# A decoder trunk on one core: TensorE's order in the first attention, and bias vectors made on 128 partitions

## The chip, the cores and the metric

The kernel runs on one core of a Trainium2 chip. The metric is device time in microseconds (us) of the whole program, from one launch; the median of three runs is given. TensorE does the matrix products (PE in the rows; PEld are its weight loads), VectorE (DVE), ScalarE (ACT) and GpSimd (POOL) work on rows of data, SyncE (SP) issues most transfers, and ScalarE's queue issues some. [...]

## The reference

Two layers on 512 rows of 1024 numbers, in float32. The first layer's mixer is an NSA (sparse attention with three branches: compressed, selected and window) beside a DSA (an index that picks the top 256 keys, then latent attention). The second is a differential attention. After each comes an MLP with a squared ReLU. A table of 32 distances x 16 heads is added to every softmax logit.

```python
h = modulate(x, sh1, sc1)                     # sh, sc, g from c @ ada_w + ada_b
...
nsa_q, kvc, kvs, kvw, gate, dsa_q, dsa_kv, idx_q, idx_k, idx_w = _split(h @ w_in, EVEN_SIZES)
o_a = nsa_attention(nsa_q, kvc, kvs, kvw, gate, ..., rel_bias[:, :NSA_HEADS])
o_b = dsa_attention(dsa_q, dsa_kv, idx_q, idx_k, idx_w, kv_norm, w_uk, w_uv, rel_bias[:, NSA_HEADS:])
y = jnp.concatenate([o_a, o_b], axis=-1) @ w_out
x = layer_norm(ALPHA * x + (1.0 + g1[:, None, :]) * y, ln_g[l, 0], ln_b[l, 0])
h = modulate(x, sh2, sc2)
y = jnp.square(jax.nn.relu(h @ w1)) @ w2
```

## The kernel before

Every float32 product with a weight is made as three matmuls of rounded numbers (`mm3`, L348 to L352): a value is kept as a high part (a cast, on ScalarE, L265) and a low part (value minus high part, on VectorE, L266), and high x high, high x low and low x high are added up in a PSUM bank.

`even` (L1030) is the first attention. It runs in these stages:

- **First projection** (L1045 to L1062): eight steps k. Step k loads a slice of ada_w and of ev_b1, makes `mod`, the high part of `hT` on ScalarE (L1051) and the low part on VectorE, and issues 24 matmuls of 512 columns and the like, into eight banks. The bias vectors are made in the meantime (`bias_vectors`, L587): `go` multiplies the table with a matrix of ones and zeros in five matmuls (L603), on 16 and 8 rows of output, and copies them to SBUF; `write` sends them to DRAM on ScalarE's queue, as `bvec` (16 heads, each repeated 23 times, 640 numbers) and `bdec` (8 heads, 8 times). It is called at k == 7, after the `hT` of that step. The repeats give every partition its own shifted copy when SyncE reads `g` from `bvec` (L537) and `ot` from `bdec` (L1214): those are the tables that are added to the scores.
- **Evacuation**: the key of the index and three of its four pairs of queries (`ik`, `iq`) are split into high and low parts (L372, L373, L472, L473), the values and the latent rows are copied (L529, L531, L1088), and `latent` (L1092 to L1100) normalizes the latent rows on VectorE; `latent_t` transposes them on TensorE (L1106).
- **A loop of 51 slots** (L1315). In each slot stand, in this order of the program: in the first 24, one unit of index scores (`idx`, scores at L504 and L505, VectorE's weighting at L1152 to L1157); then, from slot 15 on, NSA's units. Unit n has scores in slot n (`s0`: L504, L505, then the biased maximum on VectorE, L514), the division on GpSimd or VectorE one slot later (`s1`, L1277), the transposes two slots later (`s2`, L1479) and the products with the values four slots later (`pv`, L1297, L1305). Between these `fill.run` issues pieces of a queue, the **fill**: the remaining projections in the order iq, ks, kw, n0 to n3, kc, vc, the compression, and the DSA queries dq; `fill.share` says how much of it a slot gets. `topk` (L1183, L1184) adds rounds of VectorE's search for the largest index scores.
- **DSA** (L1375 to L1462): what is left of the fill, the products of the latent rows (`kproj`, Vd), and 16 units of the same kind, with the output projection of NSA's heads (eight pieces of 24 matmuls) as their fill.

The order of the instructions on each engine isn't that of the program. A scheduler walks the program and gives each engine the earliest instruction that is ready by its own model; so a matmul of the fill that stands later in the program is drawn ahead of scores that wait. Each engine's finished list is then fixed, and the chip runs it in that order.

SyncE loads weights 512 KB at a time into four buffers (`early_89`, `early_90`, `raw0_75`, `raw1_76`, L134). A buffer is free when the cast and the subtraction that read it are done, and SyncE's queue holds the loads in a fixed order, among them the loads of `g`.

Of the kernel before, what the change touches and what calls it, by code (L numbers as in the profile page):

```python
# [79 lines left out]
NREP = 23  # L80
# [207 lines left out]

class Fill:
# [37 lines left out]
class Trunk:  # L327
    def __init__(self, tc, a, out):
        self.tc, self.nc, self.a, self.out = tc, tc.nc, a, out
        self.lo_engine = "vector"  # L330
# [85 lines left out]
    def ada_pair(self, l, m, r0, r1):  # L416

        nc, mm = self.nc, self.nc.tensor.matmul
# [11 lines left out]
    def row(self, col, pool, tag, bufs=1):  # L430
# [3 lines left out]
        for h in range(2):  # L434
            ps = self.bank(self.row_tag)
            for k in range(4):
                c = 4 * h + k
                nc.tensor.matmul(ps[:, 128 * k:128 * k + 128], lhsT=col[:, c:c + 1].to_broadcast([128, 128]), rhs=self.ident,
                                 start=True, stop=True)
# [62 lines left out]
    def scores(self, ps, q, k, qs, ks, start=True):  # L502
        mm = self.nc.tensor.matmul
# [83 lines left out]
    def bias_vectors(self):  # L587
# [112 lines left out]
    def ln_b_(self, t, h, rows):  # L700

        nc, (_, cols) = self.nc, rows
        for kk in range(2):
            p = self.bank("t", (128, 4, 128))
            for k in range(4):
                nc.tensor.transpose(p[:, k, :], h[kk][:, 128 * k:128 * k + 128], self.ident)
# [323 lines left out]
    def even(self):  # L1030
# [14 lines left out]
        for k in range(8):  # L1045
# [14 lines left out]
            if k == 7:  # L1060
# [41 lines left out]
        def latent_t():  # L1102
            pt = self.bank("t")
            for t in range(4):
                ts = slice(128 * t, 128 * t + 128)
                nc.tensor.transpose(pt[:, ts], kv[:, ts], self.ident)  # L1106
# [112 lines left out]
        def cmp_a(k, i):  # L1219
# [6 lines left out]
            for s in range(4):  # L1226
                for o in range(0, 128, m):
                    nc.tensor.matmul(ps[o:o + m, 32 * s:32 * s + 32], lhsT=f32(nq[4 * k + s])[:, 128 * i + o:128 * i + o + m],
# [21 lines left out]
        def cmp_c(k, i, cb):  # L1250
            pt = self.bank("t")
            nc.tensor.transpose(pt[:, :128], cb, self.ident)
# [34 lines left out]
        def pv(n):  # L1287
# [6 lines left out]
            for br in range(2):  # L1294
                for j in range(i + 1):
                    for ab in range(2):
                        nc.tensor.matmul(o[ab], lhsT=V[:, br, j, 64 * ab:64 * ab + 64], rhs=pts[ab][br][:, 128 * j:128 * j + 128],  # L1297
# [16 lines left out]
        self.phase = "n"  # L1314
        for slot in range(end):  # L1315
# [74 lines left out]
        def s0(n):  # L1390
# [6 lines left out]
            for ab in range(2):  # L1397
                ps = self.bank("s")
                if i:
                    nc.tensor.matmul(ps[:, :w], lhsT=self.negr, rhs=drop[i][:, :w], start=True, stop=False)  # L1400
# [18 lines left out]
        def pv(n):  # L1419
# [3 lines left out]
            if p == 3:  # L1423
                po = self.bank("o")[:, :128]
                for j in range(i + 1):
                    c = (0, 128, 0, 384)[i] + 128 * j
                    for ab in range(2):
                        nc.tensor.matmul(po[64 * ab:64 * ab + 64], lhsT=Vd[:, j, p, 64 * ab:64 * ab + 64], rhs=PT[p][ab][:, c:c + 128],
# [16 lines left out]
        for n in range(N + e3):  # L1445
# [16 lines left out]
            st.pump(6)  # L1462
        self.phase = None
# [6 lines left out]
    def to_pt(self, i, zs, pts, c=None):  # L1470
# [5 lines left out]
        for z in zs:  # L1476
            t = self.bank("t")
            for j in range(i + 1):
                self.nc.tensor.transpose(t[:, 128 * j:128 * j + 128], z[:, 128 * j:128 * j + 128], self.ident)  # L1479
# [4 lines left out]
    def pv(self, po, pts, vs, half):  # L1484

        n = 4 if half else 2
        for j in range(n):
            both = j < n - 1
            for ab, (pt, v) in enumerate(zip(pts, vs)):
# [4 lines left out]
                self.nc.tensor.matmul(o if both else o[:, 128:], lhsT=v[j], rhs=y, start=j == 0, stop=j == n - 1)  # L1494
# [16 lines left out]
    def compress(self, kc, vc):  # L1511
# [4 lines left out]
        for kv in range(2):  # L1516
# [3 lines left out]
            for c in range(4):  # L1520
                w = st.get(I["cw1", kv, c])
                for li in range(4):
                    for k in range(2):
                        cs = 256 * li + 128 * k
                        for o in (0, 64) if 1 else (0,):
                            m = 64 if 1 else 128
                            nc.tensor.matmul(pss[k][o:o + m], lhsT=w[:, cs + o:cs + o + m], rhs=xl[:, :, 4 * c + li],
# [23 lines left out]
            for k in range(2):  # L1551
                if kv == 0:
                    nc.tensor.matmul(ps[:, :64], lhsT=w2[:, 128 * k:128 * k + 128],
# [369 lines left out]
```

## Time and profile before

| | |
|---|---|
| median of 3 runs | 1448.98 us (1446.71 to 1451.75) |
| the profiled execution | 1449.99 us; span of its instructions 1448.2 us |
| granted clock of TensorE, mean | 0.966 |
| VectorE busy | 1143.5 us (79%) |
| ScalarE busy | 658.8 us (45%) |
| GpSimd busy | 581.0 us (40%) |
| transfers | 189.47 MB, 131 GB/s on average |
| chain that ended last | TensorE 67%, VectorE 19%, DMA 4%, issue 4%, ScalarE 3%, GpSimd 2% |

A row of a timeline gives the start in us, how long the instruction or the group took, the engine and line, and in brackets how long the engine had been idle before and what ended that ("<-DVE q L373": it waited for VectorE's instruction of that line). [...] The profiled execution lies 1.0 us above the median.

### The profile page before, as it was taken

The page shows a single profiled execution, that of the slowest core. Times are in us where ns is not written, and L with a number is a line of the kernel's source. Part 1 is how long each engine was busy: PE and PEld are TensorE (multiplying, and loading weights), DVE is VectorE, ACT ScalarE, POOL GpSimd, SP SyncE. Part 2 cuts the span into 40 slices and gives each one's busy share as a digit, 9 for nine tenths or more (in the row PEclk, how much of TensorE's full clock was granted, in tenths as well). Part 3 has the DMA queues.
Part 4 walks back from the last instruction along what each step waited for, and adds up shares of the span by engine and source line. Part 5 has one row for each costly group of instructions (what it writes and reads, how often), then busy time and mean ns, then how long its engine had stood idle before and what let it go on. Part 6 is the DMA issues. An engine that isn't in the chain of part 4 may idle for free.

```text
span 1448.2 us, 22535 instructions
## 1 busy us (share of the span) xinstructions
PE 1342.0 (93%) x8286; PEld 1124.3 (78%) x8286; DVE 1143.5 (79%) x2185; ACT 658.8 (45%) x1412; POOL 581.0 (40%) x432
## 2 busy tenths in 40 slices
PE   6979998899899999999999799999979899999985
PEld 4758666676589888888887687887769789999974
DVE  6678979767578778878789825888975997898898
ACT  2455565746355333333332536776565443333321
POOL 2242677716432444444453622124164523122234
PEclk9989999999999999999999899999989999999997
DMA  9852432423731554444542442332350233323311
GB/s 333 247 165 94 152 104 90 131 72 106 258 132 37 183 178 172 175 175 161 189 163 91 149 153 92 102 103 78 137 166 14 90 100 117 110 70 113 116 59 58
DMA packets 58625, 189.47 MB, mean 131 GB/s; under 512 B 7778, under 2 KB 8482, under 8 KB 58516
## 3 DMA queue, kind: packets, MB, share of 16 engines
q1 hardware_dynamic: 55840, 184.67, 37.5%
q10 hardware_dynamic: 2676, 3.38, 1.1%
q8 instruction: 65, 1.06, 0.3%
q14 instruction: 44, 0.36, 0.1%
HBM read 178.42 MB, written 9.60 MB: 130 GB/s over the span
## 4 chain that ended last, share of the span: by engine, by line
PE 67%; DVE 19%; DMA 4%; issue 4%; ACT 3%; POOL 2%; SPq 0%; DVEq 0%; ACTq 0%; POOLq 0%
PE ps_mm L350 9%; PE ps_mm L351 9%; PE ps_mm L352 9%; PE ps_o L350 4%; PE ps_o L351 4%; PE ps_o L352 4%; PE ps_s L350 3%; PE ps_s L351 3%; PE ps_s L352 3%; PE ps_t L352 2%; PE ps_t L350 2%; PE ps_t L351 2%; DVE b L266 2%; PE ps_s L504 2%; PE ps_o L1297 2%
## 5 line engine op out<-in xcount | busy, mean ns | idle before, releaser
L350 PE MATMUL ps_mm<-hT,b 128*128 128x256 f32 (+1 forms) x560 | 190.9, 343 | 19.2 <-ACT b L265 13.1
L351 PE MATMUL ps_mm<-hT,b 128*128 128x256 f32 (+1 forms) x560 | 189.5, 339 | 5.4 <-DVE hT L717 5.1
L352 PE MATMUL ps_mm<-hT,b 128*128 128x256 f32 (+1 forms) x560 | 188.7, 338 | 1.8 <-DVE b L220 1.8
L350 PEld LDWEIGHTS ps_mm<-hT,b 128*128 128x128 f32 x560 | 108.5, 194 | 35.3 <-ACT b L265 13.1
L351 PEld LDWEIGHTS ps_mm<-hT,b 128*128 128x128 f32 x560 | 108.7, 194 | 18.1 <-DVE hT L717 5.6
L220 POOL TENSOR_TENSOR b<-s,b 128x512 fp32r<-128x512 f32 x33 | 46.9, 1423 | 183.6 <-ACT b L219 179.7
L517 ACT ACTIVATE z<-z,st 128x128 f32<-128x128 f32 (+3 forms) x160 | 89.3, 559 | 65.2 <-DVE st L514 56.5
L896 POOL TENSOR_TENSOR ot<-z,ot 128x512 fp32r<-128x512 f32 x39 | 61.3, 1572 | 141.4 <-ACT ot L895 127.8
L352 PEld LDWEIGHTS ps_mm<-hT,b 128*128 128x128 f32 x560 | 108.3, 194 | 12.0 <-DVE b L220 2.0
L350 PE MATMUL ps_o<-b,ot 128*128 128x512 f32 x251 | 101.1, 403 | 4.0 <-ACT b L265 2.3
L351 PE MATMUL ps_o<-b,ot 128*128 128x512 f32 x251 | 99.9, 398 | 2.9 <-DVE b L266 2.9
L731 DVE TENSOR_TENSOR u<-ps_o,u 128x512 f32<-128x512 f32 x121 | 82.3, 680 | 22.9 <-PE ps_o L352 22.6
L352 PE MATMUL ps_o<-b,ot 128*128 128x512 f32 x251 | 99.3, 396 | 0.0
L514 DVE CUSTOM_DVE_ANT_0 z<-ps_s,g 128x128 f32<-128x128 f32 (+3 forms) x160 | 75.2, 484 | 24.6 <-PE ps_s L505 19.0
L265 ACT CAST b<-raw 128x1024 fp32r<-128x1024 f32 (+1 forms) x62 | 64.3, 1042 | 61.6 <-issue 14.4
L266 DVE TENSOR_TENSOR b<-s,b 128x1024 fp32r<-128x1024 f32 x47 | 70.6, 1505 | 18.7 <-ACT b L265 18.3
L265 ACT CAST b<-s 128x1024 fp32r<-128x1024 f32 x47 | 49.0, 1048 | 78.1 <-PE ps_t L351 15.8
L266 DVE TENSOR_TENSOR b<-raw,b 128x1024 fp32r<-128x1024 f32 (+1 forms) x42 | 55.3, 1318 | 33.6 <-ACT b L265 33.3
L350 PE MATMUL ps_s<-b,ot 128*128 128x512 f32 x181 | 72.8, 402 | 0.0
L351 PE MATMUL ps_s<-b,ot 128*128 128x512 f32 x181 | 72.0, 398 | 0.0
L731 DVE TENSOR_TENSOR u<-ps_s,u 128x512 f32<-128x512 f32 x87 | 59.2, 681 | 15.8 <-PE ps_s L352 15.6
L352 PE MATMUL ps_s<-b,ot 128*128 128x512 f32 x181 | 71.6, 396 | 0.0
(471 smaller groups left out, 4241.4 us busy)
## 6 DMA issues: line engine op xcount, KB each, us to landing
s<-mlp_w SPq DMA_DIRECT2D x55, 512.0 KB
s<-ada_p SPq DMA_DIRECT2D x39, 512.0 KB
s<-mlp_wp SPq DMA_DIRECT2D x33, 512.0 KB
raw<-ada_w SPq DMA_DIRECT2D x23, 512.0 KB
raw<-mlp_w SPq DMA_DIRECT2D x21, 512.0 KB
raw<-mlp_wp SPq DMA_DIRECT2D x19, 512.0 KB
early<-ada_w SPq DMA_DIRECT2D x17, 512.0 KB
raw<-ada_p SPq DMA_DIRECT2D x17, 512.0 KB
```

Of the source, the lines that this page charges most:

```text
L220: (nc.gpsimd if PLAN["sl"][it.l][n] else nc.vector).tensor_tensor(out=lo, in0=src, in1=f32(hi), op=ALU.subtract)
L265: nc.scalar.copy(out=hi.cols(c.start, w), in_=raw[:, c])
L266: getattr(nc, ("vector", "gpsimd")[PLAN["lo"][it.name]] if it.name in PLAN["lo"] else k.lo_engine).tensor_sub(out=lo.cols(c.start, w), in0 ...
L350: mm(ps, lhsT=l[0], rhs=r[0], start=start, stop=False)
L351: mm(ps, lhsT=l[0], rhs=r[1], start=False, stop=False)
L352: mm(ps, lhsT=l[1], rhs=r[0], start=False, stop=stop)
L504: mm(ps, lhsT=q[:, qs], rhs=k[0][:, ks], start=start, stop=False)
L514: i = nc.vector.tensor_tensor_reduce(out=z[:, :w], in0=ps, in1=bias, scale=-1.0, scalar=3e38, op0=ALU.add, op1=ALU.min, accum_out=st[:, m: ...
L517: j = nc.scalar.activation(out=z[:, :w], in_=z[:, :w], func=AF.Exp, scale=-1.0, bias=st[:, m:m + 1], accum_out=st[:, 2 + m:3 + m])
L731: self.nc.vector.tensor_add(out=u[:, sl], in0=ps, in1=u[:, sl])
L896: (nc.gpsimd if PLAN["hl"][l][f % 2] else nc.vector).tensor_tensor(out=hl[:, c0:c1], in0=r[:, c0:c1], in1=f32(hh[:, c0:c1]), op=ALU.subtract)
L1297: nc.tensor.matmul(o[ab], lhsT=V[:, br, j, 64 * ab:64 * ab + 64], rhs=pts[ab][br][:, 128 * j:128 * j + 128], start=i % 2 == 0 and br == 0 ...
```

## The change

Two parts, in one diff.

1. **The order.** A new class `InOrder` stands between the kernel and TensorE. While its flag is on, each matmul or transpose gets a dependence on the one before it in the program that makes the scheduler keep that order, and costs no semaphore. The flag is on from the slot loop of `even` to the end of its DSA loop. Every call of `nc.tensor` goes through it.
2. **The bias vectors.** The 24 columns of the table are first repeated eight times by one copy on VectorE (`rep`), so that the five matmuls give 128 or 64 rows, each head eight times. `bvec` then has 24 repeats and is written from 128 partitions, three pieces of 2560 bytes each, and `bdec` from 64 partitions. `write` is called at k == 6, so it stands on ScalarE ahead of step 7.

```diff
-NREP = 23
+NREP = 24
...
+class InOrder:
+    def __init__(self, tc):
+        self.tc, self.pe, self.on, self.last = tc, tc.nc.tensor, False, None
+
+    def put(self, i):
+        if self.on and self.last is not None:
+            self.tc.add_manual_dep(i.ins, self.last.name,
+                                   mybir.DependencyInfo(mybir.DependencyClass.NoSync, mybir.DependencyReason.DATA), reason="in order")
+        self.last = i.ins
+        return i
+
+    def matmul(self, *a, **kw):
+        return self.put(self.pe.matmul(*a, **kw))
...
     def mm3(self, ps, l, r, start, stop):
-        mm = self.nc.tensor.matmul
+        mm = self.pe_.matmul
...
-        sb = [self.s4()[:16, :HB] for _ in range(2)]
+        sb = [self.s4()[:, :HB] for _ in range(2)]
 
         def go():
+
+            rep = self.z()[:33, :192]
+            nc.vector.tensor_copy(out=rep.rearrange("p (m r) -> p m r", r=8), in_=tab[:, :, None].to_broadcast([33, 24, 8]))
...
-                nc.tensor.matmul(p[:m, :n], lhsT=tab[:, t0:t0 + m], rhs=oh[i][:, c0:c0 + n], start=True, stop=True)
-                nc.vector.tensor_copy(out=sb[i][:m, c0:c0 + n], in_=p[:m, :n])
+                self.pe_.matmul(p[:8 * m, :n], lhsT=rep[:, 8 * t0:8 * t0 + 8 * m], rhs=oh[i][:, c0:c0 + n],
+                                 start=True, stop=True)
+                nc.vector.tensor_copy(out=sb[i][:8 * m, c0:c0 + n], in_=p[:8 * m, :n])
+
         def write():
-            nc.scalar.dma_start(out=self.bvec, in_=sb[0][:, None, :NVEC].to_broadcast([16, NREP, NVEC]))
-            for x, c in ((sb[0][:8, NVEC:], slice(0, HB - NVEC)), (sb[1][:8], slice(HB - NVEC, 16 * NDEC))):
-                nc.scalar.dma_start(out=self.bdec[:, :, c], in_=x[:, None, :].to_broadcast([8, 8, x.shape[1]]))
+            c = NREP // 8
+            nc.scalar.dma_start(out=self.bvec.rearrange("h (r c) n -> (h r) c n", c=c),
+                                in_=sb[0][:, None, :NVEC].to_broadcast([128, c, NVEC]))
+            for x, c in ((sb[0][:64, NVEC:], slice(0, HB - NVEC)), (sb[1][:64], slice(HB - NVEC, 16 * NDEC))):
+                nc.scalar.dma_start(out=self.bdec.rearrange("h r n -> (h r) n")[:, c], in_=x)
...
-            if k == 7:
+            if k == 6:
                 with self.tc.issue_after(act.ins):
                     bias_write()
...
         self.phase = "n"
+        self.pe_.on = True
         for slot in range(end):
...
             st.pump(6)
+        self.pe_.on = False
```

In all, 1299 of TensorE's 7463 entries stand elsewhere, all of them between the places 27 and 1593 of its list; behind that the lists are alike. The others move with them: 301 entries on ScalarE, 112 on GpSimd, 72 of SyncE's 392.

On ScalarE, at the end of the first projection, the order was this (`s4_158` and `s4_159` hold the bias vectors; `hT_111<-z_341` is the hT of k = 6, `hT_111<-z_378` that of k = 7):

```order
L1051 ACTIVATE hT_111<-z_341,mod_113 128x4x128
L265 CAST b20_81<-raw1_76 128x928
L1051 ACTIVATE hT_111<-z_378,mod_113 128x4x128
L606 DMA bvec_156<-s4_158 368x1x640
L608 DMA bdec_157<-s4_158 64x1x208
L608 DMA bdec_157<-s4_159 64x1x848
L265 CAST b30_83<-early_89 128x1024
L248 ACTIVATE early_90,adac_124<-early_90 128x1024
```

and is now:

```order
L1079 ACTIVATE hT_111<-z_343,mod_113 128x4x128
L633 DMA bvec_156<-s4_158 384x1x640
L636 DMA bdec_157<-s4_158 64x208
L636 DMA bdec_157<-s4_159 64x848
L265 CAST b20_81<-raw1_76 128x928
L1079 ACTIVATE hT_111<-z_380,mod_113 128x4x128
L248 ACTIVATE early_90,adac_124<-early_90 128x1024
L265 CAST b30_83<-early_89 128x1024
```

The three transfers have moved ahead of the last cast and the last hT of the first projection.

On SyncE, in the queue of loads behind the first projection (`g_...` are the tables read from bvec, `ev_b2` weights of the fill), the order was this:

```order
L134 DMA raw1_76<-ev_b2 128x1024
L134 DMA early_90<-ev_b2 128x1024
L134 DMA early_89<-ada_w 128x1024
L537 DMA g_1001<-bvec_156 128x1x512
L134 DMA raw0_75<-ada_w 128x1024
L537 DMA g_1003<-bvec_156 128x1x512
L134 DMA raw1_76<-ada_w 128x1024
```

and is now:

```order
L134 DMA raw1_76<-ev_b2 128x1024
L558 DMA g_1003<-bvec_156 128x1x512
L558 DMA g_1005<-bvec_156 128x1x512
L134 DMA early_90<-ev_b2 128x1024
L134 DMA early_89<-ada_w 128x1024
L134 DMA raw0_75<-ada_w 128x1024
L1393 DMA u_2854<-x 128x1024
```

Both loads of g have moved ahead of the last piece of ev_b2; `raw1_76<-ada_w` now follows behind `u`.

On TensorE, where NSA passes into DSA (`ps_t`: transposes of NSA's last units, `ps_o`: their products with the values, `ps_mm`: projections, `ps_s_2897` and `ps_s_2899`: the first scores of DSA), the order was this:

```order
L1297 MATMUL ps_o_2623<-s4_2592,V_506 64x128
L1297 MATMUL ps_o_2623<-s4_2630,V_506 64x128
L1305 MATMUL ps_o_2623<-ot_1980,ot_1428 64x256 x2
L350 MATMUL ps_mm_2878<-b10_79,k_900 128x512
L351 MATMUL ps_mm_2878<-b11_80,k_900 128x512
L352 MATMUL ps_mm_2878<-b10_79,k_901 128x512
L504 MATMUL ps_s_2897<-k_2864,q_2161 128x128
L505 MATMUL ps_s_2897<-kl_476,q_2161 128x128
L504 MATMUL ps_s_2900<-k_2865,q_2162 128x128
L505 MATMUL ps_s_2900<-kl_477,q_2162 128x128
L1479 MATMUL ps_t_2706<-ident_130,z_2614 128x128 x3
L1297 MATMUL ps_o_2738<-s4_2658,V_506 64x128
```

and is now (every product is made in one helper, so all lines read L303):

```order
L303 MATMUL ps_mm_2814<-hT_111,b00_77 128x512
L303 MATMUL ps_mm_2814<-hT_112,b00_77 128x512
L303 MATMUL ps_mm_2814<-hT_111,b01_78 128x512
L303 MATMUL ps_mm_2862<-k_902,b10_79 128x512
L303 MATMUL ps_mm_2862<-k_903,b10_79 128x512
L303 MATMUL ps_mm_2862<-k_902,b11_80 128x512
L303 MATMUL ps_mm_2875<-b10_79,k_902 128x512
L303 MATMUL ps_mm_2875<-b11_80,k_902 128x512
L303 MATMUL ps_mm_2875<-b10_79,k_903 128x512
```

All transposes and products of NSA now stand ahead of these rows. The first three shown are the last of the 24 matmuls of `ps_mm_2814`, the last projection of dq, of which none stood here before; DSA's first scores, `ps_s_2899`, follow nine matmuls behind the last row.

## Rows read from the trace of the kernel before

**Rows 1.** The page, part 1: busy time, share of the span, instructions.
```profile
PE 1342.0 (93%) x8286; PEld 1124.3 (78%) x8286; DVE 1143.5 (79%) x2185; ACT 658.8 (45%) x1412; POOL 581.0 (40%) x432
```

**Rows 2.** Windows (us): TensorE, its weight loads, VectorE, ScalarE, GpSimd busy; granted clock, DMA.
```profile
16.00:59.00 43.00, 42.68 (x195) 34.88 (x195) 34.19 (x60) 15.33 (x19) 6.87 (x3) 1.00 0.92 307
...
90.00:127.00 37.00, 36.77 (x232) 30.12 (x232) 26.39 (x47) 17.82 (x35) 6.25 (x5) 0.92 0.36 108
127.00:184.00 57.00, 52.69 (x417) 41.70 (x416) 54.28 (x161) 29.93 (x75) 30.39 (x28) 0.94 0.43 141
184.00:214.00 30.00, 27.69 (x203) 19.33 (x201) 22.39 (x79) 18.69 (x52) 21.96 (x21) 0.89 0.28 93
214.00:258.00 44.00, 40.31 (x265) 30.98 (x264) 43.08 (x135) 24.93 (x67) 33.11 (x31) 0.96 0.30 101
258.00:282.00 24.00, 20.47 (x147) 14.63 (x145) 17.22 (x54) 18.82 (x53) 17.48 (x18) 0.93 0.34 112
282.00:310.00 28.00, 27.12 (x182) 20.54 (x183) 19.89 (x50) 13.97 (x34) 10.68 (x9) 1.00 0.36 120
```

**Rows 3.** Chain of waits from 60 to 200 us: start, us, what.
```profile
49.48 11.88 DMA bvec<-s
61.38 4.04 SPq L537
...
66.86 9.87 DMA raw<-ada_w
...
89.39 0.70 DVE ot L473
90.23 0.76 PE ps_mm L350
```

**Rows 4.** Timeline of ScalarE, 44 to 75 us.
```profile
49.48 0.82 ACT L1051 ACTIVATE hT<-z,mod 128x512 fp32r<-128x512 f32 x1 [2.08 <-DVE mod L1049]
49.48 0.68 ACTq L606 DMA_DIRECT2D bvec<-s  x1
50.20 5.58 ACTq L608 DMA_DIRECT2D bdec<-s  x2
55.90 1.05 ACT L265 CAST b<-early 128x1024 fp32r<-128x1024 f32 x1 [5.60 <-issue]
...
67.94 1.05 ACT L265 CAST b<-early 128x1024 fp32r<-128x1024 f32 x1 [7.09 <-DMA early<-ev_b]
```

**Rows 5.** Timeline of SyncE's queue.
```profile
58.02 0.33 SPq L134 DMA_DIRECT2D early<-ev_b  x1
```

**Rows 6.** Windows of 2 us, columns as in rows 2; the last two are DMA share, GB/s.
```profile
52.00:54.00 2.00, 2.00 (x10) 1.69 (x10) 1.29 (x2) 0.00 (x0) 0.31 (x1) 1.00 1.04 318
54.00:56.00 2.00, 2.00 (x11) 1.84 (x11) 0.00 (x0) 0.10 (x1) 0.00 (x0) 1.00 0.93 114
...
66.00:68.00 2.00, 2.00 (x6) 1.53 (x5) 0.00 (x0) 0.06 (x1) 0.00 (x0) 0.50 0.74 268
```

**Rows 7.** Timeline of TensorE, 53 to 94 us.
```profile
54.39 0.61 PE L350 MATMUL ps_mm<-hT,b 128*128 128x512 f32 x2
...
56.23 0.39 PE L351 MATMUL ps_mm<-hT,b 128*128 128x512 f32 x1
56.46 0.40 PE L352 MATMUL ps_mm<-hT,b 128*128 128x512 f32 x1
...
86.63 0.91 PE L1106 MATMUL ps_t<-ident,ot 128*128 128x128 f32 x3 [6.32 <-DVE ot L1099]
```

**Rows 8.** Waits from 61 to 370 us, of TensorE and VectorE: us, times, longest.
```profile
PE ps_s L504 <- DVE st L514: 9.7, 9, 2.5
...
DVE z L514 <- PE ps_s L505: 9.4, 13, 2.0
...
DVE s L529 <- PE ps_t L1479: 5.4, 8, 1.4
```

**Rows 9.** Timeline of VectorE: one copy.
```profile
63.15 0.41 DVE L529 COPY V<-ps_o 128x256 f32<-128x256 f32 x1
```

More of the change, by code (lines that the diff above doesn't have):

```diff
@@ L286, in pump, with transpose @@
                 self.process()
+class InOrder:
[9 more added lines that the diff above has]
+        return self.put(self.pe.matmul(*a, **kw))
+    def transpose(self, *a, **kw):
+        return self.put(self.pe.transpose(*a, **kw))
 class Fill:
@@ L329, in __init__ @@
         self.tc, self.nc, self.a, self.out = tc, tc.nc, a, out
+        self.pe_ = InOrder(tc)
         self.lo_engine = "vector"
@@ L416, in ada_pair @@
     def ada_pair(self, l, m, r0, r1):
-        nc, mm = self.nc, self.nc.tensor.matmul
+        nc, mm = self.nc, self.pe_.matmul
         ps = self.bank(self.ada_tag)
@@ L437, in row @@
                 c = 4 * h + k
-                nc.tensor.matmul(ps[:, 128 * k:128 * k + 128], lhsT=col[:, c:c + 1].to_broadcast([128, 128]), rhs=self.ident,
+                self.pe_.matmul(ps[:, 128 * k:128 * k + 128], lhsT=col[:, c:c + 1].to_broadcast([128, 128]), rhs=self.ident,
                                  start=True, stop=True)
@@ L502, in scores @@
     def scores(self, ps, q, k, qs, ks, start=True):
-        mm = self.nc.tensor.matmul
+        mm = self.pe_.matmul
         mm(ps, lhsT=q[:, qs], rhs=k[0][:, ks], start=start, stop=False)
@@ L705, in ln_b_ @@
             for k in range(4):
-                nc.tensor.transpose(p[:, k, :], h[kk][:, 128 * k:128 * k + 128], self.ident)
+                self.pe_.transpose(p[:, k, :], h[kk][:, 128 * k:128 * k + 128], self.ident)
             m = self.ot(F32).rearrange("p (k t) -> p k t", k=4)
@@ L1105, in latent_t @@
                 ts = slice(128 * t, 128 * t + 128)
-                nc.tensor.transpose(pt[:, ts], kv[:, ts], self.ident)
+                self.pe_.transpose(pt[:, ts], kv[:, ts], self.ident)
             box["ck"] = (k2(), k2())
@@ L1251, in cmp_c @@
             pt = self.bank("t")
-            nc.tensor.transpose(pt[:, :128], cb, self.ident)
+            self.pe_.transpose(pt[:, :128], cb, self.ident)
             self.copy(i, pc[k][:, 128 * i:128 * i + 128], pt[:, :128])
@@ L1399, in s0 @@
                 if i:
-                    nc.tensor.matmul(ps[:, :w], lhsT=self.negr, rhs=drop[i][:, :w], start=True, stop=False)
+                    self.pe_.matmul(ps[:, :w], lhsT=self.negr, rhs=drop[i][:, :w], start=True, stop=False)
                 self.scores(ps[:, :w], dq[p][ab], dk[p][ab], slice(128 * i, 128 * i + 128), slice(0, w), not i)
@@ L1478, in to_pt @@
             for j in range(i + 1):
-                self.nc.tensor.transpose(t[:, 128 * j:128 * j + 128], z[:, 128 * j:128 * j + 128], self.ident)
+                self.pe_.transpose(t[:, 128 * j:128 * j + 128], z[:, 128 * j:128 * j + 128], self.ident)
             ts.append(t)
@@ L1493, in pv @@
                 o = po[64 * ab:64 * ab + 64]
-                self.nc.tensor.matmul(o if both else o[:, 128:], lhsT=v[j], rhs=y, start=j == 0, stop=j == n - 1)
+                self.pe_.matmul(o if both else o[:, 128:], lhsT=v[j], rhs=y, start=j == 0, stop=j == n - 1)
     def compress_in(self, ps, kv):
@@ L1552, in compress @@
                 if kv == 0:
-                    nc.tensor.matmul(ps[:, :64], lhsT=w2[:, 128 * k:128 * k + 128],
+                    self.pe_.matmul(ps[:, :64], lhsT=w2[:, 128 * k:128 * k + 128],
                                      rhs=h[:, k, 0].rearrange("p g n -> p (g n)"), start=k == 0, stop=k == 1)
                 else:
-                    nc.tensor.matmul(ps[:, :64], lhsT=h[:, k].rearrange("p d g n -> p (d g n)"),
+                    self.pe_.matmul(ps[:, :64], lhsT=h[:, k].rearrange("p d g n -> p (d g n)"),
                                      rhs=w2[:, 256 + 64 * k:320 + 64 * k], start=k == 0, stop=k == 1)
@@ L1673, in s2 @@
             for j in range(i + 1):
-                nc.tensor.transpose(t[:, 128 * j:128 * j + 128], z[:, 128 * j:128 * j + 128], self.ident)
+                self.pe_.transpose(t[:, 128 * j:128 * j + 128], z[:, 128 * j:128 * j + 128], self.ident)
             pts[n] = self.s2("q")
@@ L1685, in s3 @@
                 v = V[h // 4][j // 2][:, 512 * (j % 2) + c:512 * (j % 2) + c + 128]
-                nc.tensor.matmul(po[h][:, i], lhsT=pt[:, js], rhs=v, start=j == 0, stop=j == i)
+                self.pe_.matmul(po[h][:, i], lhsT=pt[:, js], rhs=v, start=j == 0, stop=j == i)
             if i == 3 or h == 7:
@@ L1716, in s5 @@
                 c = slice(128 * i, 128 * i + 128)
-                nc.tensor.transpose(t[:, c], o[:, c], self.ident)
+                self.pe_.transpose(t[:, c], o[:, c], self.ident)
             if len(ot) == h:
```

10 lines of the change are left out of this document (5 added, 5 removed).

## The prediction

> **What bounds the kernel now.** I read the page's busy times first, then the windows of the first attention, the chain of waits from 60 us on, and the timelines of the engines that the chain names. TensorE is busy for 1342.0 of 1448.2 us [rows 1], so a change that leaves TensorE's work as it is can only shorten its waits and its stretches at half clock. The windows [rows 2] show where these lie: from 90 to 127 us TensorE works through (36.77 of 37); in NSA, 127 to 282 us, it is idle 4.31 + 2.31 + 3.69 + 3.53 = 13.8 us, with mean clocks of 0.89 to 0.96; from 282 to 310, where NSA passes into DSA, only 0.88 us. VectorE is busy 54.28 of 57 and 43.08 of 44 us in 127 to 184 and 214 to 258: these two stretches are VectorE's.
>
> Ahead of that the chain [rows 3] runs through the write of the bias vectors (11.88 us), 4.04 us in SyncE's queue, a load of ada_w (9.87 us) issued behind it, and VectorE's latent work, until TensorE takes up its third projection of the fill at 90.23. ScalarE's timeline [rows 4] shows the same from its side: the write goes out at 49.48, right after the last hT; the two issues of bdec take 5.58 us and leave ScalarE idle for 5.60; later it waits 7.09 us for a load of ev_b2 that SyncE issued at 58.02 [rows 5] and that landed near 67.9, and the evacuations of the index queries stand behind that wait. While bvec and bdec are written out of 16 and 8 partitions, the DMA engines read as 0.93 busy and move 114 GB/s; just before, with loads to 128 partitions in flight, 318 [rows 6].
>
> **The bias part, term by term.** The five matmuls and five copies keep their columns (only their partitions grow from 16 and 8 to 128 and 64), so I take them at no change. One DVE copy is added (33 x 192); nearest row: a copy of 256 columns took 0.41 us [rows 9]. It stands ahead of the bias matmuls, which TensorE mixes into the first projection, where VectorE has 43 - 34.19 = 8.8 idle us [rows 2]; I cost it at 0, and at 0.4 with that cover gone.
>
> The write of bvec grows from 368 pieces to 384, 920 KB to 983. Bounds: as slow as now, 11.88 us x 384/368 = 12.4; or at 318 GB/s, 3.1. I take 4, because its source is now of the kind that made the 318. It also starts a step earlier: the last hT came late by its mod (idle 2.08 [rows 4]), so the write goes out after the hT of k=6, near 46 instead of 49.5. The cast and the hT of k=7 now stand behind its issues on ScalarE: with the whole stall of today hT ends some 5.6 us later, near 55.9, and TensorE reaches k=7 at 54.39 [rows 7]. The price with the cover gone is thus 1.5 us. I take 0, because a write that drains in 4 us should not hold the queue for 5.6.
>
> What follows: bvec is there near 50 instead of 61.4. SyncE's two loads of g, now ahead of early<-ev_b2 in its queue, find it there. The load of ev_b2 then starts some 4 us earlier, and its cast on ScalarE now stands behind the evacuations of the first two pairs of index queries instead of ahead of them. The load of ada_w, the one on the chain, may go when VectorE has read the buffer's last content, near 61.7 instead of 66.86: 5.2 us earlier. Its 9.87 us [rows 3] fell among the tail of bdec and other loads; without the tail I take 7, between 2 (512 KB at the 268 GB/s of [rows 6]) and 9.87. So VectorE's latent work, its evacuation at 89.39 and with it TensorE's projection at 90.23 come 5.2 + 2.9 = **8 us** earlier. Bounds: 4 (same landing time, and ScalarE's cast ahead of that buffer 1 us later) and 11. From 90 to 127 TensorE is never idle, so the gain arrives at NSA's first unit.
>
> [...]
>
> **The order part.** It moves 1299 of TensorE's instructions and adds none. Three moves count.
> 1. The first index scores, which today go out in a bunch when the second projection is nearly done, stand after every 12 matmuls of it. The evacuations that they need come earlier by the bias part; else TensorE would stand before them with the fill behind. The four latent transposes go 114 places back; today TensorE waits 6.32 us for them [rows 7]. That is inside the 8 us above, since the projection behind them waits for VectorE's 89.39 as well, so I add nothing.
> 2. In NSA each unit's scores come ahead of its fill. With the mean durations of its rows, TensorE has 6.6, 3.5, 9.6 and 6.5 us less to do ahead of the scores of units 8, 16, 24 and 31. VectorE waited 9.4 us for scores and 5.4 for transposes [rows 8]. Of this the stretches that VectorE bounds can give back no more than its idle time in them, 2.72 + 0.92 = **3.6 us**, and I take that. In the other two it is idle 7.6 + 6.8 = 14.4 us, but there ScalarE, GpSimd and TensorE take turns; with those 14.4 the gain would be 18, its far bound. VectorE's own order has 2.8 us more ahead of unit 0, which its 10.6 idle us between 90 and 127 hide [rows 2].
> 3. The fill is no longer drawn into TensorE's gaps. The last dq projection, 24 matmuls that today lie among the units, now stands between NSA's last product and DSA's first scores. 24 x 0.23 us (the spacing of two such matmuls [rows 7]) = **5.5 us** land in 282 to 310, where TensorE has 0.88 us free. Less work in NSA doesn't shorten what VectorE bounds there, so I take all of it. [...]
>
> Sum of the order part: 5.5 - 3.6 = +1.9, from -18 to +8.5.
>
> [...]
>
> **The sum.** 1449.99 (profiled run) - 8 + 1.9 = 1443.9. The median of the three runs, 1448.98, is 1.0 lower, so I forecast **1443 us**. After DSA's fourth unit TensorE has had the same work before and after, and what follows moves along.
>
> **Rivals.**
> - *The order gives more* (chance 0.17): VectorE's waits for TensorE go in the mixed stretches too. For it: the scores come ahead by most exactly there. Half of the 14.4 us: 1443 - 7 = 1436.
> - *The deferred fill eats the gain* (0.24): units are no faster, since each still waits on VectorE, and the 5.5 us and a held-up hT (1.5) come due: 1449 - 8 + 5.5 + 1.5 = 1448, no change. For it: VectorE's 95 and 98% of two stretches. Against: its waits for scores stand in the rows.
> - *Waits in order* (0.19): slower. Place: NSA's scores. TensorE waited 9.7 us in 9 places for VectorE to free a score bank [rows 8]; with scores ahead of the fill, what ran in the meantime now stands behind them. Twice as many such waits cost 9.7 more, and 3 of half clock: 1443 + 12.7 = 1455.7. It decides, against before, once these waits grow by 6 us.
> - *The write isn't faster* (0.10): bvec lands near 58 all the same, and the loads of ev_b2 and ada_w wait behind g. Then only the 3.5 us of the earlier start are left, against which stand 1.9 and a late hT of 1.5: 1449.
>
> The forecast itself has 0.30. A measurement of this kernel can tell about 0.3%, 4.3 us, from no change: below 1444.6 is faster, above 1453.3 slower. The forecast and the first rival make most of faster, 0.47; the second and fourth and the forecast's upper edge most of no change, 0.34; the third makes slower, 0.19. The range, **1432 to 1456**, goes from below the first rival to the third.
>
> **What would show it.** Right: bvec written in 3 to 5 us; ScalarE's stall gone, or over before TensorE's k=7; the third projection of the fill near 82; unit 0 near 119; NSA 3 to 4 us shorter and its passage to DSA 5 longer. Wrong: the write still near 100 GB/s; hT of k=7 late; TensorE's waits for a score bank well over 9.7 us; more half clock from 110 to 280 us; or a DSA that starts no earlier than now.

## The result, and the profile after

| | before | changed kernel |
|---|---|---|
| median, same chip | 1447.85 us (4 runs) | 1467.20 us (4 runs, 1464.76 to 1471.78) |
| ratio | 1 | 1.0137, 95% interval 1.0105 to 1.0169 |
| profiled execution | 1449.99 us | 1471.78 us, span 1470.0 |
| mean granted clock | 0.966 | 0.953 |

The change makes the kernel slower, by some 20 us. The profiled executions lie 2.1 and 4.6 us above their medians, so the rows below differ by two or three us more than the medians do. Busy times of the engines in the changed kernel, to be held against [rows 1]:

```profile
PE 1333.0 (91%) x8286; PEld 1126.2 (77%) x8286; DVE 1145.0 (78%) x2186; ACT 661.6 (45%) x1412; POOL 577.9 (39%) x432
```

No engine has notably more to do, as forecast; the span is longer by 21.8 us of waiting. (Behind the new class, lines of the changed kernel lie 20 to 30 further on; L303 and L306 are the helper through which every matmul and transpose goes.)

**The bias part does what was said.** ScalarE's timeline at the end of the first projection, against [rows 4]:

```profile
44.57 0.61 ACTq L633 DMA_DIRECT2D bvec<-s  x1
45.22 2.31 ACTq L636 DMA_DIRECT2D bdec<-s  x2
47.65 0.97 ACT L265 CAST b<-raw 128x928 fp32r<-128x928 f32 x1 [2.27 <-issue]
48.53 0.81 ACT L1079 ACTIVATE hT<-z,mod 128x512 fp32r<-128x512 f32 x1
...
61.07 1.04 ACT L265 CAST b<-early 128x1024 fp32r<-128x1024 f32 x1 [0.36 <-DMA early<-ev_b]
```

The write goes out at 44.57 instead of 49.48. Its issues hold ScalarE for 2.27 us, not 5.60, and the hT of k=7 ends at 49.3 (48.53 + 0.81), well before the 54.39 at which TensorE took up that step in the kernel before [rows 7]. The wait of 7.09 us for ev_b2 is 0.36. How the write moves is seen in ScalarE's queue (q10: packets, MB, and the time of its packets as a share of 16 DMA engines). The changed kernel, from 48 to 50 us:

```profile
q10 hardware_dynamic: 170, 0.39, 66.0%
```

and the kernel before, from 54 to 58 us:

```profile
q10 hardware_dynamic: 167, 0.43, 94.5%
```

From 16 and 8 partitions, 0.43 MB took 94.5% of all DMA engines for 4 us; from 128 and 64, 0.39 MB took 66% of them for 2 us, and loads took another 33% (q1 in the same 2 us).

**Then the time is lost in NSA and behind it.** The next two fences are windows (columns as in [rows 2]) cut at the same events in both kernels, by VectorE's timeline: first scores of NSA's unit 0, of unit 8, of the last unit 31, of DSA's unit 0 and of its last unit. Before:

```profile
127.20:184.30 57.10, 52.79 (x416) 41.80 (x415) 54.54 (x161) 30.23 (x75) 30.41 (x29) 0.94 0.43 140
184.30:279.50 95.20, 86.46 (x599) 63.81 (x599) 79.94 (x262) 59.74 (x165) 72.10 (x68) 0.93 0.30 100
279.50:289.60 10.10, 8.43 (x53) 5.45 (x52) 8.72 (x19) 7.56 (x17) 6.46 (x6) 1.00 0.56 162
289.60:359.70 70.10, 66.60 (x402) 51.61 (x402) 47.68 (x131) 38.88 (x101) 27.23 (x25) 1.00 0.29 90
sum 232.50, PE 214.28 PEld 162.68 DVE 190.88 ACT 136.41 POOL 136.19; mean PE 53.57 PEld 40.67 DVE 47.72 ACT 34.10 POOL 34.05
```

The changed kernel:

```profile
122.10:187.50 65.40, 46.98 (x389) 37.31 (x389) 55.67 (x172) 27.38 (x72) 30.66 (x29) 0.84 0.38 120
187.50:286.60 99.10, 81.92 (x615) 65.14 (x615) 74.91 (x243) 54.81 (x154) 53.66 (x59) 0.86 0.20 65
286.60:316.90 30.30, 23.97 (x161) 17.60 (x160) 10.89 (x21) 17.88 (x34) 19.31 (x13) 0.89 0.49 156
316.90:380.70 63.80, 58.41 (x336) 45.77 (x335) 46.80 (x134) 38.23 (x101) 31.90 (x26) 1.00 0.34 101
sum 258.60, PE 211.29 PEld 165.82 DVE 188.27 ACT 138.30 POOL 135.53; mean PE 52.82 PEld 41.46 DVE 47.07 ACT 34.58 POOL 33.88
```

Unit 0 comes 5.1 us earlier. NSA (the first two rows) then takes 164.5 us instead of 152.3, the passage to DSA, from the scores of NSA's last unit to DSA's first ones, 30.3 instead of 10.1, and DSA gives 6.3 back. TensorE's busy time is nearly the same, 211.3 and 214.3; what grew is its idle time, 258.6 - 211.3 = **47.3 us instead of 18.2**, and the mean granted clock in NSA fell from 0.94 and 0.93 to 0.84 and 0.86. Its waits say on what; from unit 0 to DSA's first scores, changed kernel (us in total, times, longest):

```profile
PE ps_t L306 <- POOL z L1275: 13.7, 4, 7.6
PE ps_o L303 <- ACT raw L248: 7.1, 1, 7.1
PE ps_o L303 <- DVE ot L1579: 5.1, 1, 5.1
PE ps_mm L303 <- DVE q L494: 4.5, 1, 4.5
PE ps_mm L303 <- DVE z L1260: 3.1, 1, 3.1
PE ps_s L303 <- ACT z L1229: 2.8, 8, 0.5
PE ps_o L303 <- ACT z L1568: 1.5, 1, 1.5
...
PE ps_s L303 <- DVE st L535: 0.9, 2, 0.5
```

The wait for VectorE to free a score bank of [rows 8], 9.7 us, is down to 0.9, with 2.8 for ScalarE to free one. In its place stand waits of the **compressed branch**: its transposes (13.7 us, for GpSimd's product z) and the second products of the compression (7.1 + 5.1). Two more are for banks that this branch holds: a projection of the fill waits 3.1 us until VectorE has read the compressed scores, and a product with the values 1.5 until ScalarE has read the compression's first product. In the kernel before, TensorE has no wait of over 1.2 us between the same events but those for score banks. A row names the releaser that came last by the profile, and that can be the wrong one, as with the first wait (a row of ScalarE, one of VectorE, one of TensorE):

```profile
130.50 1.04 ACT L248 ACTIVATE raw<-raw 128x1024 f32<-128x1024 f32 x1
131.57 0.21 DVE L1579 TENSOR_SCALAR ot<-z 128x124 f32<-128x124 f32 x1
131.88 1.08 PE L303 MATMUL ps_o<-ot 128*128 128x64 f32 x4 [7.13 <-ACT raw L248]
```

The operand is `ot`, and VectorE's L1579 wrote it, ready at 131.78: the last of a chain of small steps on VectorE and ScalarE that stand among VectorE's other work. ScalarE's L248 makes no part of it.

### The profile page after: what moved, and what is told of

Its sections match the earlier page's. It is cut to its first block, busy times and chain, and to the rows that moved or that the text cites. A ratio compares the mean times of both kernels' runs of the same rounds, so it can differ in the third digit from the quotient of the medians.

```text
span 1470.0 us, 22529 instructions
## 1 busy us (share of the span) xinstructions
PE 1333.0 (91%) x8286; PEld 1126.2 (77%) x8286; DVE 1145.0 (78%) x2186; ACT 661.6 (45%) x1412; POOL 577.9 (39%) x432
## 4 chain that ended last, share of the span: by engine, by line
PE 63%; DVE 17%; DMA 7%; ACT 4%; POOL 4%; issue 4%; DVEq 0%; SPq 0%; ACTq 0%; POOLq 0%
PE ps_mm L303 27%; PE ps_o L303 14%; PE ps_s L303 14%; PE ps_t L303 7%; PE ps_t L306 2%; DVE b L266 2%; DVE u L759 2%; POOL b L266 2%; DMA raw<-ev_b 1%; DMA raw<-ev_out 1%; ACT b L265 1%; DMA s<-mlp_w 1%; POOL raw L247 1%; DVE ot L1212 1%; DVE z L535 1%
## 5 line engine op out<-in xcount | busy, mean ns | idle before, releaser
L303 PE MATMUL ps_mm<-hT,b 128*128 128x256 f32 (+1 forms) x1680 | 334.3, 345 | 30.5 <-ACT b L265 13.3
L303 PEld LDWEIGHTS ps_mm<-hT,b 128*128 128x128 f32 x1680 | 267.1, 197 | 67.5 <-ACT b L265 13.3
L303 PE MATMUL ps_o<-b,ot 128*128 128x512 f32 x753 | 201.6, 398 | 6.9 <-DVE b L266 2.9
L303 PEld LDWEIGHTS ps_o<-b,ot 128*128 128x128 f32 x753 | 134.7, 190 | 35.4 <-DVE b L266 3.6
L303 PE MATMUL ps_s<-b,ot 128*128 128x512 f32 x543 | 146.7, 398 | 0.0
L303 PEld LDWEIGHTS ps_s<-b,ot 128*128 128x128 f32 x543 | 99.1, 192 | 18.6 <-issue 0.8
L303 PE MATMUL ps_mm<-b,ot 128*128 128x512 f32 x384 | 101.0, 411 | 5.1 <-DVE u L759 5.0
L303 PEld LDWEIGHTS ps_mm<-b,ot 128*128 128x128 f32 x384 | 72.7, 196 | 22.5 <-DVE u L759 6.8
L266 DVE TENSOR_TENSOR b<-s,b 128x1024 fp32r<-128x1024 f32 x47 | 70.6, 1505 | 18.9 <-ACT b L265 18.8
L266 DVE TENSOR_TENSOR b<-raw,b 128x1024 fp32r<-128x1024 f32 (+1 forms) x42 | 56.8, 1353 | 32.4 <-ACT b L265 32.2
L306 PE MATMUL ps_t<-ident,z 128*128 128x128 f32 x360 | 61.1, 289 | 19.2 <-POOL z L1275 13.7
L306 PEld LDWEIGHTS ps_t<-ident,z 128*128 128x128 f32 x360 | 43.8, 146 | 37.4 <-POOL z L1275 15.9
L266 POOL TENSOR_TENSOR b<-raw,b 128x1024 fp32r<-128x1024 f32 x20 | 47.6, 2384 | 55.9 <-ACT b L265 51.8
L303 PEld LDWEIGHTS ps_t<-q,b 128*128 128x128 f32 x504 | 66.3, 188 | 4.3 <-issue 0.4
```

The source lines that it names most:

```text
L266: getattr(nc, ("vector", "gpsimd")[PLAN["lo"][it.name]] if it.name in PLAN["lo"] else k.lo_engine).tensor_sub(out=lo.cols(c.start, w), in0 ...
L303: return self.put(self.pe.matmul(*a, **kw))
L306: return self.put(self.pe.transpose(*a, **kw))
```

## The experiments

Two theories at first: the order costs and the bias part gains (A), or the bias part costs (B). Then, inside the order, which instructions cost. All kernels are the changed one with an edit; ratios are against the kernel before on the same chip.

**The bias part alone** (no order):

```diff
-        self.pe_.on = True
+        self.pe_.on = False
         for slot in range(end):
```

> The changed kernel with the order's flag never on, so only the bias part of the change is left. Theory A (the order costs, the bias part gains): some 1442 us, 6 under before, with unit 0 of NSA near 120 us and the passage from NSA's last scores to DSA's first near 10 us, as before. Theory B (the bias part, by loads that now collide, is what costs): 1455 or more. If both parts gain nothing alone: 1448.

Measured: 1440.11 us, ratio 0.9946 (0.9920 to 0.9971). Its windows, at the same events:

```profile
121.20:180.90 59.70, 51.15 (x408) 40.20 (x408) 55.55 (x162) 29.03 (x74) 29.39 (x28) 0.94 0.41 131
180.90:271.70 90.80, 86.89 (x625) 63.90 (x623) 77.06 (x257) 60.88 (x166) 70.04 (x68) 0.98 0.34 105
271.70:279.60 7.90, 6.64 (x45) 4.59 (x46) 6.74 (x17) 6.64 (x14) 6.15 (x5) 1.00 0.67 210
```

Unit 0 at 121.2 and a passage of 7.9 us: theory A. Theory B falls.

**The order alone** (bias vectors on 16 and 8 partitions, written after k=7):

```diff
-            if k == 6:
+            if k == 7:
...
-        sb = [self.s4()[:, :HB] for _ in range(2)]
+        sb = [self.s4()[:16, :HB] for _ in range(2)]
```

> The changed kernel with the bias vectors made on 16 and 8 partitions and written after k=7, as before; the order of the program on TensorE stays. Theory A: the order's whole cost without the gain, 1467 + 5 = 1472 to 1475 us. Theory B: 1448 to 1452.

Measured: 1482.12 us, 1.0227 (1.0193 to 1.0261): 33 us slower, more than the 24 to 27 expected. Most of the distance to the changed kernel is there at NSA's first scores, which come at 133.9 us instead of 122.1. One wait makes much of it: TensorE stands 13.0 us before an index score whose query is evacuated late, with the fill behind it in the order. In the changed kernel, where the bias part brings the evacuation forward, it is 4.7.

**The order off behind the slot loop:**

```diff
+        self.pe_.on = False
         fill.flush()
...
-        self.pe_.on = False
```

> The changed kernel with the flag off again after the slot loop, so the last dq projection, the latent projections and DSA are free to move. The 24 matmuls of dq and their evacuation leave the passage; 15 matmuls stay in it. Theory A1 (two thirds of the loss arise in the passage, where TensorE works 39 matmuls with waits between, 30 us instead of 10): the passage shrinks to 15 to 20 us and the time to 1455 to 1458. Theory A2 (the loss arises in NSA and the passage only shows it): 1465 to 1468.

Measured: 1466.47 us, 1.0123 (1.0088 to 1.0158), no less than the changed kernel. The passage did shrink, from 30.3 to 23.0 us, but NSA's last unit came 2.6 us later and DSA's last one at 380.0 instead of 380.7. The time is that of theory A2; the passage shrank by less than A1 said. It looks as if work is only shifted from one side of the passage to the other, as long as NSA is slow and its fill is left over.

**The compressed branch out of the order:**

```diff
-                    self.pe_.matmul(ps[o:o + m, 32 * s:32 * s + 32], lhsT=f32(nq[4 * k + s])[:, 128 * i + o:128 * i + o + m],
+                    nc.tensor.matmul(ps[o:o + m, 32 * s:32 * s + 32], lhsT=f32(nq[4 * k + s])[:, 128 * i + o:128 * i + o + m],
...
-            self.pe_.transpose(pt[:, :128], cb, self.ident)
+            nc.tensor.transpose(pt[:, :128], cb, self.ident)
...
-                    self.pe_.matmul(ps[:, :64], lhsT=w2[:, 128 * k:128 * k + 128],
+                    nc.tensor.matmul(ps[:, :64], lhsT=w2[:, 128 * k:128 * k + 128],
```

> The changed kernel with four kinds of TensorE instruction taken out of the order, all of the compressed branch: its scores, its transposes (which wait for GpSimd) and the second products of the compression. Theory A (these are the places where TensorE stands still with work behind it: 29 us of waits from 122 to 282 us): the waits for GpSimd's z and for the compression fall under 8 us and NSA's last unit comes 8 to 12 us earlier, time 1456 to 1460. If VectorE bounds NSA anyway and the waits only stand where others stood: 1465 to 1468.

Measured: 1458.32 us, 1.0071 (1.0044 to 1.0099), inside the expected 1456 to 1460. Windows from unit 8 on:

```profile
177.50:270.40 92.90, 78.22 (x615) 61.38 (x615) 71.41 (x242) 53.71 (x151) 52.56 (x60) 0.93 0.23 69
270.40:304.90 34.50, 26.81 (x164) 19.86 (x163) 13.29 (x24) 17.92 (x35) 20.91 (x13) 0.83 0.42 138
```

NSA's last unit comes at 270.4, 16 us earlier than in the changed kernel (8 to 12 were expected) and 1.3 earlier than in the bias part alone. The second products no longer wait; the transposes still do, for 9.6 us, more than the 8 in all that was expected. But the passage now takes 34.5 us with 26.8 of work, much of it fill that wasn't done in NSA.

**Where in the program:** the order kept in the first 15 slots only, and from slot 15 on only:

```diff
             n = slot - X0
+            if n == 0:
+                self.pe_.on = False
```

(In the second kernel the flag goes on at `n == 0` and not ahead of the loop.)

> The changed kernel with the order kept only in the first 15 slots (index scores and fill ahead of NSA's units); from slot 15 on the scheduler is free. Theory B1 (the order costs only from NSA on, where scores, transposes and products wait and the fill is held behind them): within 4 us of the bias part alone, 1437 to 1444. Theory B2 (TensorE's waits ahead of NSA, 4.7 + 4.6 us for the index queries, carry on to the end): 1447 to 1452.

> The counterpart: the order kept from slot 15 to the end of DSA, free before. Theory B1: 1463 to 1470, all of the loss. Theory B2: 1455 to 1460, with the first unit near 121 us as in the bias part alone.

Measured: 1440.16 us, 0.9948 (0.9928 to 0.9968), and 1474.98 us, 1.0190 (1.0160 to 1.0220). Ahead of NSA the order costs nothing that can be told; all of the loss arises from slot 15 on. That the second is slower than the changed kernel itself, over the 1470 of theory B1, was not expected and stays open; the two intervals overlap a little. Its unit 0 came 3.0 us earlier than in the changed kernel, and its NSA took 171.5 us instead of 164.5.

**The fill out of the order, and both out of it.** `fill.run`, `flush` and `force` set a flag while a piece is issued, and `put` leaves such instructions alone:

```diff
     def put(self, i):
+        if self.free:
+            return i
```

> The changed kernel with the pieces of the fill (projections, compression, in DSA the output projection) taken out of the order, while scores, transposes, products with the values and the rest keep it. Theory C1 (the cost is the fill that is held behind a waiting matmul and comes due later): TensorE's idle time from unit 0 to DSA's last unit falls from 47 us to 18 to 25, the passage to DSA to under 20 us, and the time to 1440 to 1448. Theory C2 (the cost is the order of the attention's own matmuls, each waiting for VectorE, ScalarE or GpSimd): 1458 to 1468.

> As the kernel with the fill out of the order, and the compressed branch's scores and transposes out of it too. Theory C1, if the transposes that wait for GpSimd hold nothing but attention's own work once the fill is free: within 4 us of the kernel with the fill free alone. If they still hold up scores: 4 to 10 us faster than that kernel, down to the 1440 of the bias part alone.

Measured: 1456.34 us, 1.0053 (1.0028 to 1.0079), and with the compressed branch free as well 1450.11 us, 1.0032 (1.0010 to 1.0055). So neither C1 nor C2 holds for the first. The held fill is some 12 us of the loss and the passage is 18.7 us, as C1 had it, but TensorE's idle time from unit 0 to DSA's last unit, 242.1 - 208.0 = 34.1 us, stays well over the 25 that C1 allowed, and the compressed transposes still wait 11.3.

Whether freeing the compressed branch besides gives anything is open: the second kernel is 6 us faster by the medians and 3 by the ratios, whose intervals overlap. It has NSA's last unit at 275.9, but the passage is still long:

```profile
275.90:298.00 22.10, 14.66 (x100) 11.13 (x101) 10.66 (x22) 8.66 (x17) 5.36 (x5) 0.85 0.32 111
```

These 14.7 us of work are NSA's last transposes and products and, kept behind them by the order, the 15 latent matmuls, which aren't pieces of the fill.

**And the passage free too** (the last kernel with the flag off behind the slot loop; the edit is that of the third experiment):

> The kernel with fill and compressed branch out of the order, and besides the flag off after the slot loop, so that the 15 latent matmuls may lie among NSA's last products and DSA is free. What is left in order are the scores, transposes and products of NSA. Theory D1 (of the 0.9% that the kernel with fill and compressed branch free still loses against the bias part alone, most arises in the passage, 22 us instead of 8, behind NSA's last products): the passage falls to 8 to 13 us and the time to 1438 to 1443, the same as the bias part alone. Theory D2 (the order of NSA's own matmuls costs it): 1446 to 1451.

Measured: 1443.15 us, 0.9962 (0.9940 to 0.9983).

```profile
274.80:286.70 11.90, 10.00 (x80) 7.67 (x81) 8.62 (x20) 6.69 (x14) 7.21 (x5) 0.90 0.57 163
```

The passage is back at 11.9 us (in a profiled execution that was the fastest of twelve, 4.8 us under the median), and the interval overlaps with that of the bias part alone: theory D1, with the median 0.15 us over its range. The same edit that gave nothing by itself gives 0.7% here; a likely reason, not tried by itself, is that now no left-over fill stands ahead of the latent matmuls. So the order's cost reads: 1.0137 with all of it, 1.0032 without fill and compressed branch, 0.9962 with index scores and NSA's remaining scores, transposes and products alone in order, 0.9946 with none. How it divides is rough: each edit lets the scheduler lay out the other engines' lists anew, and a new layout alone can be worth about as much as one of these steps (the 9 us below).

**The bias part taken apart** (no order): 128 partitions, written after k=7; and 16 and 8 partitions, written after k=6.

```diff
-            if k == 6:
+            if k == 7:
```

> The bias part alone on 128 partitions, but written after the hT of k=7 as before; no order. Theory P (the partitions make the gain: the write takes 4 us wherever it starts): 1440 to 1443, like the bias part alone. Theory S (the earlier start and the changed place in the queues make it): 1446 to 1449.

> The counterpart: bias vectors on 16 and 8 partitions as before, written after the hT of k=6; no order. Theory P: the write still moves some 110 GB/s and ends near 57 us, the hT of k=7 comes late behind 5.6 us of issue, SyncE's loads of g block ev_b2: 1446 to 1452. Theory S: 1440 to 1443.

Measured: 1431.13 us, 0.9881 (0.9848 to 0.9915), and 1449.33 us, 1.0003 (0.9984 to 1.0023). The partitions make the whole gain, and the earlier place none. The first is better than expected, by 9 us against the same kernel with k == 6, and is the fastest kernel of the study, ahead of both given ones. These 9 us are not won at unit 0, which comes at 123.0 us instead of 121.2, but behind it: NSA takes 143.2 us instead of 150.5. The second kernel, too, is no slower than the one before although its unit 0 comes 3.2 us later, at 130.4. To see whether the place in the queues makes the 9 us, the changed kernel, order and all, with k == 7:

> The changed kernel, order and all, with the write after the hT of k=7. TensorE's order is then that of the changed kernel but for one matmul, so a difference comes from the place of the write in the queues of ScalarE and SyncE alone. Theory Q (the place after k=6 costs by itself, since SyncE's loads of g then stand ahead of ev_b2): 0.5 to 0.8% under the changed kernel, 1455 to 1461 us. Theory R (without the order kept, moving the write makes the scheduler lay out another order for all engines, and that is what made the 9 us between the two kernels with the bias part alone): no change, 1463 to 1471.

Measured: 1466.29 us, 1.0124 (1.0105 to 1.0144), the same as with k == 6. Theory R: with TensorE's order held, the place is worth nothing. That the 9 us come from the other order that the scheduler lays out when the write moves fits this, but was not tested by itself.

This run makes a third pair for either part. The partitions gain 1.0% with the order held (1.0227 to 1.0124, both with k == 7), 1.2% without it and with k == 7, 0.6% without it and with k == 6. The order costs 1.9% in the change as given, 2.3% with the bias vectors as before, 2.4% on 128 partitions with k == 7. So the sign of neither part hangs on one layout.

## Why the prediction was wrong

- **The bias part: right in size, in part by luck.** Forecast -8 us, measured 0.54% of 1449, 7.8 us (4.2 to 11.6). The write took some 7 us and not 4 (ScalarE's queue moved 0.33, 0.39 and 0.45 MB of its 1.26 from 44 to 48, 50 and 52 us), while loads took 48%, 33% and 43% of the DMA engines' time; ScalarE's stall was over before k=7. But the 8 us were to be there when the projection of the fill that came at 90.23 [rows 3] starts, and to arrive at unit 0. That projection came at 86.08, not 82, and unit 0 at 122.1, not 119 (121.2 in the bias part alone): 4 to 6 us of the 8, within the bounds of 4 and 11. In the bias part alone NSA and the passage then gave 1.8 and 2.2 us more and DSA took 2.9 back, for none of which this part had a term; and with k == 7 the same partitions gave 17 us. The earlier start, a step of the sum, is worth nothing by itself (1.0003). (The bound of 11 should have been 13 by its own terms, 5.2 + 9.87 - 2, and 920 KB are units of 1024 bytes beside the 983 of 1000; neither moves the sum.)
- *What was missing ahead of unit 0* stands in VectorE's rows. The load of ada_w was there in time: VectorE took it up (L250) 9.5 us earlier. But the work from there on was taken to be as long as before, and it grew. The changed kernel:

```profile
67.24 3.22 DVE L250 SCALAR_TENSOR_TENSOR raw<-raw,cact 128x1024 f32<-128x1024 f32 x1
...
77.20 2.34 DVE L418 SCALAR_TENSOR_TENSOR t<-t,ss 128x4 f32<-128x4 f32 x1
79.57 2.30 DVE L419 SCALAR_TENSOR_TENSOR rk<-t 128x4 f32<-128x4 f32 x1
```

The kernel before:

```profile
76.76 1.23 DVE L250 SCALAR_TENSOR_TENSOR raw<-raw,cact 128x1024 f32<-128x1024 f32 x1 [2.29 <-DMA raw<-ada_w]
...
85.74 0.15 DVE L397 SCALAR_TENSOR_TENSOR t<-t,ss 128x4 f32<-128x4 f32 x1
85.93 0.16 DVE L398 SCALAR_TENSOR_TENSOR rk<-t 128x4 f32<-128x4 f32 x1
```

These three took 6.3 us more, each beside large operations of GpSimd: two of L247 ran from 66.98 and 69.33 us (2.40 and 3.40 us), two of L266 from 77.14 and 79.48 (2.38 and 2.37 us); see also the last section. No run takes them away, so that they make the shortfall is read from the rows alone.
- **The order part: wrong,** +1.9 forecast, within -18 to +8.5; measured 1.0137 - 0.9946 = 1.9% or 28 us. Step 1, taken at nothing, held (0.9948 with the order ahead of NSA alone). Two steps failed.
- *Step 2 of the order part* took 3.6 us as gain in NSA, what "the stretches that VectorE bounds can give back". NSA became 12.2 us longer, 14.0 against the bias part alone. The step looked at the instructions that come first by the order (scores) and at who waits for them, but not at those that now stand with the rest of the list behind them: transposes and second products of the compressed branch, whose operands come late, from GpSimd and from the chain of small steps on VectorE and ScalarE. They wait 13.7 + 7.1 + 5.1 = 25.9 us, and freeing this branch (with its scores) brought NSA's last unit forward by 16 us, though the time by only some 9, with the fill then due in the passage.
- *Step 3* priced the displaced fill at 24 matmuls without a wait, 5.5 us. The upper end of the sum, +8.5, and the price of the third rival each hold 3 us more for half clock, a term that no run shows; what the runs showed in its place is a mean granted clock of 0.84 and 0.86 in NSA and 0.89 in the passage, where it had been 0.94, 0.93 and 1.00. The passage grew by 20.2 us, 22.4 against the bias part alone. TensorE has 15.5 us more work in it (24.0 instead of 8.4), because the order holds more than that projection back: the remaining pieces of the fill, the 15 latent matmuls, of which the rows of the order named six with nine more behind, and NSA's last products. Another 4.7 us is idle: the latent matmuls wait for one evacuation after the other, and behind the first wait of 4.50 us nine of them run at half clock (granted 0.50 from 308.95 to 313.80 us; six of them take 2.93 us, 0.49 each, where the 24 of the row at 298.05, at 1.00, take 0.24 each):

```profile
298.05 5.74 PE L303 MATMUL ps_mm<-hT,b 128*128 128x512 f32 x24
303.62 0.86 PE L303 MATMUL ps_mm<-k,b 128*128 128x512 f32 x3
308.98 1.62 PE L303 MATMUL ps_mm<-b,k 128*128 128x512 f32 x3 [4.50 <-DVE q L494]
310.91 2.93 PE L303 MATMUL ps_mm<-b,k 128*128 128x512 f32 x6 [0.31 <-ACT k L510]
315.31 0.96 PE L303 MATMUL ps_mm<-b,k 128*128 128x512 f32 x3 [1.48 <-DVE Vd L550]
```

- *The base of both:* what costs is less the work that is moved than the time in which TensorE stands, with work behind that the order holds, 18.2 us before and 47.3 after. As the order was loosened it went down, to 34.1 with the fill free, 31.2 with the compressed branch free too, and 23.0 with the passage free; in the bias part alone it is 17.6. Of the signs that the prediction named as wrong, two came: more half clock (a mean of 0.84 and 0.86 in NSA) and a DSA that starts no earlier, 27 us later in fact.
- **The rival "waits in order" had the mechanism,** with a chance of 0.19 and 12.7 us, but the wrong place: score banks, where the waits went down to 0.9 + 2.8 us. Its price should have been worked out for every kind of matmul in a slot. The trace shows the mechanism in four waits before transposes of the compressed branch, 13.7 us in all (7.6, 2.9, 1.9 and 1.3): behind the longest, which ends at 230.33, stand four score matmuls and three of a projection, and none of them goes ahead of it. "The deferred fill eats the gain" was half of the truth, at a quarter of the size.
- From 16 and 8 partitions the row of the queue shows 0.43 MB in 4 us, 107 GB/s; from 128 and 64, 0.39 MB in 2 us, 195 GB/s, with loads beside it. No run here separates what 64 partitions get.

## What to carry to other kernels

The fixed order was paid for at the instructions whose operands came last (25.9 us of waits before transposes and second products of the compressed branch), not at those that it brought forward (0.9 us of waits for VectorE to free a score bank): for each kind of instruction in it, ask who makes its operand, when, and what stands behind. Work that fills gaps must be free to do so: held in order it made some 12 us of the loss, and still came due later (TensorE stood 47.3 us, and 34.1 with the fill free; the passage took 30.3 us, and 18.7). And it was worth spreading the write of the bias vectors from 16 and 8 partitions over 128 and 64 even though that made it larger: it gave 0.6, 1.0 and 1.2% in three pairs of kernels, and was the only part of the change that gained. And since one moved transfer was worth 0.7% here by what seems to be the scheduler's new layout, a difference of that size between two kernels is no proof of what was edited, unless it comes again with the order held or in another pair.

## What was not expected of the hardware

Small operations of VectorE took 2.1 to 2.3 us instead of 0.10 to 0.17 while GpSimd worked on tiles of 128x1024. In the bias part alone, VectorE's timeline of the latent work:

```profile
71.01 2.31 DVE L1123 TENSOR_SCALAR ss<-ss 128x4 f32<-128x4 f32 x1
73.24 0.20 DVE L1121 TENSOR_SCALAR gates<-gates 128x96 f32<-128x96 f32 x1
73.36 2.30 DVE L405 TENSOR_SCALAR yi<-ss 128x4 int32<-128x4 int32 x1
...
76.24 2.11 DVE L412 TENSOR_TENSOR t<-yi 128x4 f32<-128x4 f32 x1
78.38 0.16 DVE L413 TENSOR_TENSOR t<-t,ss 128x4 f32<-128x4 f32 x1
```

and GpSimd's at the same time:

```profile
67.60 2.39 POOL L247 TENSOR_TENSOR raw<-raw,cact 128x1024 f32<-128x1024 f32 x1
69.96 5.67 POOL L247 TENSOR_TENSOR early<-early,cact 128x1024 f32<-128x1024 f32 x2
75.98 2.35 POOL L266 TENSOR_TENSOR b<-raw,b 128x1024 fp32r<-128x1024 f32 x1 [0.35 <-ACT b L265]
```

Three operations on four columns took 2.1 to 2.3 us each beside GpSimd's operations, and the next 0.16 after them. The two products of the row at 69.96, read singly, took 3.33 and 2.37 us and end at 73.29 and 75.63, the third at 78.33; VectorE's three end at 73.32, 75.66 and 78.35. Not every operation there is hit: one on 96 columns took 0.20, at 73.24, where one product ends and the next begins. In the kernel before, the same four operations (L1095, L384, L391, L392) took 0.10 to 0.17 us, in a stretch where GpSimd was idle. Such steps lie on the way to the evacuation that unit 0 waits for. What holds VectorE there is not shown; what the rows show is that its three operations end 0.02 to 0.03 us behind GpSimd's.
